# A decoder mixer: TensorE's order written into the source by counted distances, and own buffers for the decode state update

## The chip, the core and the metric

The kernel runs on one core of a Trainium2 chip. The metric is the device time of one execution in microseconds (us). Before the change three runs took 2486.36, 2490.62 and 2491.24 us; the median is 2490.62 us.

The engines go by their short names: PE (TensorE) multiplies matrices, DVE (VectorE) and ACT (ScalarE) do the elementwise work, POOL (GpSimd) a little of it and part of the DMA issues, SP (SyncE) issues the loads of weights. Each engine works through its own list of instructions in order. They meet through semaphores.

## What is computed

One inference step of one decoder layer for a prompt of 256 tokens and 8 single-token samples, together 264 columns. The layer is a half-step FFN, the mixer, attention to a memory, and a second half-step FFN. The change lies in the mixer:

```python
def mixer_block(h, pos, conv_buf, s0, swa_fn, lp):
    proj = h @ lp['w_in']
    qkv_c, z, b_raw, a_raw, q_s, k_s, v_s, gate_gdn, gate_swa = jnp.split(proj, offsets, -1)
    qkv_c, conv_new = causal_conv(qkv_c, conv_buf, lp['conv_w'])
    ...
    q_g = l2_normalize(q_g.reshape(B, T, GDN_HEADS, GDN_DK)) * (GDN_DK ** -0.5)
    k_g = l2_normalize(k_g.reshape(B, T, GDN_HEADS, GDN_DK))
    beta = jax.nn.sigmoid(b_raw.astype(jnp.float32))
    g = -jnp.exp(lp['gdn_A_log']) * jax.nn.softplus(a_raw + lp['gdn_dt_bias'])
    o_g, s_new = gated_delta_rule(q_g, k_g, v_g, g, beta, s0)
    o_g = rms_norm(o_g, lp['gdn_norm']) * jax.nn.silu(z)
    q_s, k_s = rope(q_s, pos), rope(k_s, pos)
    o_s, k_buf_new, v_buf_new = swa_fn(q_s, k_s, v_s, lp['swa_sinks'])
    merged = sigmoid(gate_gdn) * (o_g @ lp['w_br_gdn']) + sigmoid(gate_swa) * (o_s @ lp['w_br_swa'])
    return merged @ lp['w_out'], s_new, conv_new, k_buf_new, v_buf_new
```

For the prompt the gated delta rule is solved in chunks: for each pair of heads a chain of small matrix products, with a triangular inverse in the middle. For a sample it is one step, S = a(I - b k k^T)S + b k v^T, on a state of 128x128 per head and sample, which is read from HBM, updated and written back.

## The kernel before

**Weights.** Every weight matmul is done in three passes of half precision: weights and input are split into a high and a low part, and wh·xh, wh·xl and wl·xh are added up in PSUM (lines 192, 193, 194). Weights come in blocks of 512 KB: a DMA into `raw` (SP, 4 buffers), a cast by ACT into `wh` (line 162, 3 buffers), and the rest by DVE into `wl` (line 163, 4 buffers). A block feeds 24 matmuls of 128x264. A `wh` buffer is written again when the last matmul of the block three earlier is done.

**Mixer.** Between these stand the small steps. The combined input projection is computed in groups: `gemm_ba` (32 columns for beta and decay, lines 351 to 417), four pairs of GDN heads ("c0" to "c3": `conv_pair` computes k, q, v and z of a pair, `gdn_pair` solves the prompt's chunks, `gdn_sample` does the decode step), the window attention's projection ("s"), its prompt heads in four groups ("w0" to "w3") and its samples ("x"), and 16 gate groups. All of the mixer's evacuations multiply by `R`, the inverse root of the mean square of the input, which PE, DVE and a chain of small DVE operations produce at its start (lines 1234, 1237, 149 to 155; `rsqrt` is an integer estimate and three Newton steps).

**Small steps.** A step is one to sixteen matmuls or transposes on PE, whose result goes through ACT or DVE before the next step of the same chain. In `gdn_pair`: transposes of q, k and v (lines 489, 495, 513), decay matrices (519 to 526; the tiles `d`, `E1`, `E2`), k·k and q·k (531, 536), the inverse in four rounds (`sq`, `d`, lines 548 to 568) and two larger ones (580 to 600), the outputs (604 to 630), their norm (635 to 643) and the transposes of the result (646). In `gdn_sample`: the states are loaded into the tiles `d`, `T`, `U` and `bv` (line 661 on), multiplied (689), reduced and turned (695, 710), the new vectors go through HBM (`ud`, 714) and come back spread over all partitions into `ke` or `u` (728), POOL multiplies them by k (729), ACT scales the state (732), POOL adds (733) and stores (734).

**Order.** The framework's scheduler sets the order of the instructions on every engine from its own model of times; the source gives the order in which work becomes known to it. PSUM holds 3 banks for weight groups (`mm`), 2 for GDN steps (`gd`), 2 for window attention (`sw`) and 1 for the rest (`ev`).

## Time and profile before

| what | value |
|---|---|
| three runs, median | 2490.62 us |
| the profiled execution | 2495.04 us, span 2493.3 us |
| granted clock of PE, mean | 0.987 of full |
| PE busy | 2443.0 us, 98% |
| DVE busy | 1516.3 us, 61% |
| ACT busy | 1101.2 us, 44% |
| POOL busy | 111.3 us, 4% |
| HBM | 182 GB/s over the span |

The first FFN takes the span to about 790 us, the mixer from there to about 1600, the memory attention and the second FFN the rest. The small steps lie between 790 and 1365 us. The profile has views by engine, by stretch of time, by wait, and the list of instructions with their start times; the rows that are used stand two sections below.

### The profile page before, as it was taken

How to read it: one execution, taken by the hardware profiler on the slowest of the kernel's cores; microseconds unless marked ns; L12 is line 12 of the kernel's file. 1: busy time of each engine (PE TensorE's matmuls, PEld its weight loads, DVE VectorE, ACT ScalarE, POOL GpSimd, SP SyncE). 2: the span in 40 equal slices, each digit the busy share in tenths (PEclk: the TensorE clock that was granted, in tenths of full speed). 3: DMA queues.
4: the chain of work that ended last, by engine and by line, in shares of the span. 5: the costliest groups of instructions: out<-in, count | busy, mean ns of one | idle time of the engine just before them, and what ended most of it. 6: DMA issues, size and time to landing. Idle time of an engine off the chain costs nothing.

```text
span 2493.3 us, 47847 instructions
## 1 busy us (share of the span) xinstructions
PE 2443.0 (98%) x19804; PEld 2392.9 (96%) x19804; DVE 1516.3 (61%) x2555; ACT 1101.2 (44%) x1647; POOL 111.3 (4%) x159
## 2 busy tenths in 40 slices
PE   8999999999999999999998999999999999999997
PEld 8999999999999999998997999979999999999997
DVE  6555544555556877877575777668555544555554
ACT  5444333444444544554463455446444333444443
POOL 0000000000000002002020310000000000000000
PEclk9999999999999999998998999999999999999999
DMA  6555555555556457544453876755555556555553
GB/s 210 182 178 179 178 179 184 182 180 178 178 179 205 147 167 232 170 162 165 136 190 127 270 229 198 240 196 178 180 183 180 174 182 186 178 181 183 175 171 130
DMA packets 136090, 455.20 MB, mean 183 GB/s; under 512 B 16736, under 2 KB 22976, under 8 KB 135824
## 3 DMA queue, kind: packets, MB, share of 16 engines
q1 hardware_dynamic: 127072, 424.18, 53.7%
q0 software_dynamic: 7504, 24.65, 2.8%
q8 instruction: 155, 2.54, 0.4%
q10 hardware_dynamic: 1296, 3.31, 0.4%
q14 instruction: 63, 0.52, 0.1%
HBM read 438.02 MB, written 14.98 MB: 182 GB/s over the span
## 4 chain that ended last, share of the span: by engine, by line
PE 94%; DVE 3%; DMA 1%; ACT 1%; issue 1%; POOL 0%; ACTq 0%; SPq 0%; DVEq 0%; POOLq 0%
PE mm L192 18%; PE mm L194 18%; PE mm L193 18%; PE mx L194 11%; PE mx L192 11%; PE mx L193 11%; DVE wl L163 1%; DMA raw<-in_w_in_dram 1%; PE sw L812 1%; PE mm L1003 0%; ACT wh L162 0%; PE mm L1005 0%; PE mm L1004 0%; PE sw L839 0%; DMA d<-in_state_gdn_dram 0%
## 5 line engine op out<-in xcount | busy, mean ns | idle before, releaser
L163 DVE TENSOR_TENSOR wl<-raw,wh 128x1024 fp32r<-128x1024 f32 (+2 forms) x794 | 958.0, 1207 | 762.3 <-ACT wh L162 756.8
L162 ACT CAST wh<-raw 128x1024 fp32r<-128x1024 f32 (+2 forms) x794 | 817.3, 1030 | 1212.4 <-PE mm L193 611.8
L192 PE MATMUL mm<-xh,wh 128*128 128x264 f32 x2672 | 769.7, 289 | 14.2 <-ACT wh L162 10.9
L194 PE MATMUL mm<-xh,wl 128*128 128x264 f32 x2672 | 766.8, 288 | 3.1 <-DVE wl L163 3.0
L193 PE MATMUL mm<-xl,wh 128*128 128x264 f32 x2672 | 768.7, 288 | 0.0
L192 PEld LDWEIGHTS mm<-xh,wh 128*128 128x128 f32 x2672 | 508.9, 191 | 18.7 <-ACT wh L162 11.1
L194 PEld LDWEIGHTS mm<-xh,wl 128*128 128x128 f32 x2672 | 507.5, 190 | 7.4 <-DVE wl L163 4.6
L193 PEld LDWEIGHTS mm<-xl,wh 128*128 128x128 f32 x2672 | 508.7, 190 | 5.0 <-issue 3.8
L192 PE MATMUL mx<-xh,wh 128*128 128x264 f32 x1424 | 407.2, 286 | 0.3 <-DVE sso L719 0.3
L194 PE MATMUL mx<-xh,wl 128*128 128x264 f32 x1424 | 407.1, 286 | 0.3 <-DVE wl L163 0.3
L193 PE MATMUL mx<-xl,wh 128*128 128x264 f32 x1424 | 406.1, 285 | 0.0
L192 PEld LDWEIGHTS mx<-xh,wh 128*128 128x128 f32 x1424 | 270.7, 190 | 0.5 <-DVE sso L719 0.4
L194 PEld LDWEIGHTS mx<-xh,wl 128*128 128x128 f32 x1424 | 270.0, 190 | 0.6 <-DVE wl L163 0.6
L193 PEld LDWEIGHTS mx<-xl,wh 128*128 128x128 f32 x1424 | 270.1, 190 | 0.0
L194 PE MATMUL mm<-hh,wl 128*128 128x264 f32 x748 | 212.7, 286 | 0.0
L192 PE MATMUL mm<-hh,wh 128*128 128x264 f32 x748 | 212.4, 284 | 0.0
L193 PE MATMUL mm<-hl,wh 128*128 128x264 f32 x748 | 212.3, 284 | 0.0
L194 PE MATMUL mx<-hh,wl 128*128 128x264 f32 x660 | 187.6, 285 | 0.0
L192 PE MATMUL mx<-hh,wh 128*128 128x264 f32 x660 | 187.5, 284 | 0.0
L193 PE MATMUL mx<-hl,wh 128*128 128x264 f32 x660 | 187.4, 284 | 0.0
L193 PEld LDWEIGHTS mm<-hl,wh 128*128 128x128 f32 x748 | 140.9, 188 | 0.0
L192 PEld LDWEIGHTS mm<-hh,wh 128*128 128x128 f32 x748 | 140.6, 188 | 0.0
(562 smaller groups left out, 2867.0 us busy)
## 6 DMA issues: line engine op xcount, KB each, us to landing
raw<-in_ffn_w_dram SPq DMA_DIRECT2D x511, 512.0 KB, 3.5
raw<-in_w_in_dram SPq DMA_DIRECT2D x152, 512.0 KB, 3.6
raw<-in_w_out_dram SPq DMA_DIRECT2D x32, 512.0 KB, 3.7
raw<-in_ffn_w_dram SPq DMA_DIRECT2D x33, 256.0 KB, 2.7
raw<-in_w_br_gdn_dram SPq DMA_DIRECT2D x16, 512.0 KB, 5.0
raw<-in_w_br_swa_dram SPq DMA_DIRECT2D x16, 512.0 KB, 4.8
gd<-gt POOLq DMA_DIRECT2D x32, 132.0 KB, 3.0
tg<-gd POOLq DMA_DIRECT2D x32, 132.0 KB, 4.6
```

What stands on the lines that cost most here:

```text
L162: nc.scalar.copy(out=H, in_=raw)
L163: nc.vector.tensor_tensor(out=L, in0=raw, in1=H.bitcast(F32), op=ALU.subtract)
L192: nc.tensor.matmul(acc, wh, xh, start=(kg + c == 0), stop=False)
L193: nc.tensor.matmul(acc, wh, xl, start=False, stop=False)
L194: nc.tensor.matmul(acc, wl, xh, start=False, stop=(kg + c == nk - 1))
L812: nc.tensor.matmul(ps[j % 2][:, a // 2], self.qr[half, 2 * g + j // 2, qs], self.kd[g][half, 0:W], start=True, stop=True)
```

## The change

- PE's order. While `te.on` is set, each matmul and transpose is kept on PE in the order of the source. The order on DVE, ACT, POOL and SP is still the scheduler's.
- Lanes. `gdn_pair`, `gdn_sample`, `gemm_ba`, `swa_prompt` and `swa_sample` become generators. `gemm` calls `tick()` after every three weight matmuls; at a tick at most one step of one lane is put into the program, and not sooner than two ticks after the last. A bare `yield` asks for 7 ticks (lane A: GDN and `gemm_ba`), 8 (lane B: window attention) or 6 (lane V: the transposes of v) to the next step, a number asks for so many.
- Program. "c0 c1 s w0 w1 c2 w2 w3 g2 x c3 g10" takes the place of "c0 c1 s c2 w0 c3 w1 x w2 w3" and 12 gate groups. `gemm_ba` now follows k of the first pair, and its steps start 24 ticks later.
- Decode state update. The states go into `S0`, `S1`, `E1`, `bv`. `ub` gets two buffers of its own. The multiplication by k moves from POOL (16 of 128x512) to ACT (64 of 128x128). The states are loaded in `gdn_pair`.
- Smaller edits: `rsqrt` loses one DVE operation; `kb` is copied from PSUM by ACT first; the transposes of v move behind q·k; rotated queries are written in place into `os`; the caches of `swa_sample` are loaded some steps ahead.

```diff
+        self.te = InOrder(tc)
+        self.clock, self.last, self.lanes = 0, 0, []
...
-        nc.vector.tensor_scalar(out=v, in0=v, scalar1=-0.5, scalar2=None, op0=ALU.mult)
         for it in range(3):
-            nc.vector.tensor_tensor(out=t, in0=y, in1=y, op=ALU.mult)
+            nc.vector.scalar_tensor_tensor(out=t, in0=y, scalar=-0.5, in1=y, op0=ALU.mult, op1=ALU.mult)
...
+                    self.te.matmul(acc, wl, xh, start=False, stop=(kg + c == nk - 1))
+                    self.tick()
...
+    def tick(self):
+        self.clock += 1
+        ready = [n for n in self.lanes if n.todo and n.at <= self.clock]
+        if ready and self.clock >= self.last + 2:
+            min(ready, key=lambda n: n.at).step()
+            self.last = self.clock
...
-                self.gemm_ba(win, xs)
                 self.conv_state_load()
-                for step in "c0 c1 s c2 w0 c3 w1 x w2 w3".split():
+                self.te.on = True
+                A, B, V = self.lanes = [Lane(self, 7), Lane(self, 8), Lane(self, 6)]
+                self.lane_v = V
+                A.add(self.gemm_ba(win, xs), 24)
+                for step in "c0 c1 s w0 w1 c2 w2 w3 g2 x c3 g10".split():
                     k = int(step[1:] or 0)
                     if step[0] == "c":
-                        self.conv_pair(win, xs, k)
-                        self.gdn_pair(k)
-                        self.gdn_sample(k)
+                        A.drain(2)
+                        q = self.conv_pair(win, xs, k)
+                        A.add(self.gdn_pair(k, q))
+                        A.add(self.gdn_sample(k, q))
...
         ot = self.gt("d")
         TT(out=ot, in0=po, in1=bc(rn, P), op=ALU.mult)
+        yield 18
...
-                S = self.gt(("d", "T", "U", "bv")[h * 2 + hb])
+                S = self.gt(("S0", "S1", "E1", "bv")[h * 2 + hb])
...
-                ub = self.gt(("ke", "u")[hb])
+                ub = self.mc.tile([P, 4, P], F32, name="ub", bufs=2)
...
-                nc.gpsimd.tensor_tensor(out=ub, in0=ub, in1=bc(kq[:, h, hb, :, 0], P), op=ALU.mult)
                 for b in range(4):
                     bb = hb * 4 + b
+                    nc.scalar.mul(out=ub[:, b], in_=ub[:, b], mul=kq[:, h, hb, b, 0:1])
                     nc.scalar.mul(out=S[:, b], in_=S[:, b], mul=self.sbg[:, 1, 2 * p + h, bb:bb + 1])
...
             pT = mc.tile([P, nh, blk + 1, P], F32, name="pT")
+            yield 18
...
+class InOrder:
+    def matmul(self, *a, **k):
+        ins = self.tc.nc.tensor.matmul(*a, **k)
+        return self.tc.keep_in_program_order(ins) if self.on else ins
...
+class Lane:
+    def add(self, gen, wait=0):
+        if not self.todo:
+            self.at = max(self.at, self.b.clock + wait)
+        self.todo.append(gen)
+
+    def step(self):
+        try:
+            n = next(self.todo[0])
+            self.at = self.b.clock + (n or self.gap)
+        except StopIteration:
+            self.todo.pop(0)
```

What this does to the order is shown at three places.

**Place 1, PE at the mixer's start.** `mm_8952` and `mm_9064` are `gemm_ba`'s sums, the matmul with `nacc` is the one that `R` begins with, `mm_9079` and `mm_9080` before and `mm_8967` and `mm_8968` after are k of the first pair, `mm_9227` and `mm_9174` the group that follows. Before:

```order
L364 MATMUL mm_8952<-xl_8914,wh_8948 32x264
L194 MATMUL mm_9080<-xh_7797,wl_9083 128x264
L192 MATMUL mm_9079<-xh_7975,wh_9112 128x264
L1234 MATMUL ev_8986<-nacc_7608,ones_74 128x264
L193 MATMUL mm_9079<-xl_7976,wh_9112 128x264
...
L194 MATMUL mm_9080<-xh_8913,wl_9173 128x264
L369 MATMUL ev_9006<-idn_73,cy_8985 128x32
L370 MATMUL ev_9006<-idn_73,cy_8985 128x32
L371 MATMUL ev_9006<-idn_73,cy_8985 8x32
L192 MATMUL mm_9227<-xh_7604,wh_9230 128x264
```

After:

```order
L1332 MATMUL mm_9064<-xl_8913,wh_9060 32x264
L1332 MATMUL ev_9099<-nacc_7607,ones_74 128x264
L1332 MATMUL mm_8967<-xh_8718,wh_9119 128x264
...
L1332 MATMUL mm_8968<-xh_8912,wl_9120 128x264
L1332 MATMUL mm_9174<-xh_7603,wh_9177 128x264
```

Before, 71 weight matmuls stood between the matmul that `R` begins with and the first PE instruction that needs `R` (the transposes of `cy`); now 24 stand between it and `mm_9174`, which is written into the bank that an evacuation with `R` must empty first.

**Place 2, DVE around the norm of pair 0's output.** `d_9915` before and `d_10618` after is the normed output that PE then transposes; `wl_11619` is of the block that PE is in the middle of at that step, `wl_10837` of the third block behind the one that PE ends on there. Before:

```order
L154 TENSOR_TENSOR got_9901<-got_9901,so_9892 128x4
L751 TENSOR_TENSOR cth_11455<-cth_11455,c_8940 128x264
L752 TENSOR_TENSOR cy_11453<-cy_11453,c_8940 128x264
...
L163 TENSOR_TENSOR wl_11619<-raw_11617,wh_11618 128x1024
L778 TENSOR_TENSOR qr_11029<-cy_11463,cth_11465 128x264
L153 TENSOR_TENSOR got_9901<-goy_9900 128x4
...
L641 TENSOR_TENSOR rn_9893<-rn_9893,tq_9894 128x4
L643 TENSOR_TENSOR d_9915<-gd_9877,rn_9893 128x512
```

After:

```order
L154 SCALAR_TENSOR_TENSOR got_10605<-goy_10604 128x4
L164 TENSOR_TENSOR wl_10837<-raw_10835,wh_10836 128x1024
L812 TENSOR_TENSOR kd2_10652<-cy_10643,cth_10645 64x264 x2
L812 TENSOR_TENSOR kd3_10656<-cy_10643,cth_10645 64x264
L155 TENSOR_TENSOR got_10605<-got_10605,so_10596 128x4
L812 TENSOR_TENSOR kd3_10656<-cy_10643,cth_10645 64x264
...
L156 SCALAR_TENSOR_TENSOR rn_10597<-got_10605,goy_10604 128x4
L681 TENSOR_TENSOR rn_10597<-rn_10597,tq_10598 128x4
L683 TENSOR_TENSOR d_10618<-gd_10581,rn_10597 128x512
```

On PE, 115 weight matmuls stood between the last product of that pair and these transposes, and 54 stand there now. The 54 end with the last that read `wh_10693`, whose buffer `wh_10836` takes.

**Place 3, PE at the end of pair 3.** `gd` and `T`, `U`, `bv`, `S` are that pair's steps, `mm` a gate. Before, where no weight matmul stands between the first and the last of these rows:

```order
L599 MATMUL gd_13760<-Pm_13758,T_13729 64x64 x4
L604 MATMUL gd_13767<-bv_13615,U_13730 128x128 x2
L608 MATMUL gd_13771<-U_13730,kb_13608 128x128 x2
L614 MATMUL gd_13777<-u_13766,ke_13606 128x128 x2
...
L628 MATMUL gd_13794<-u_13766,ke_13606 128x128 x2
L646 MATMUL gd_13827<-idn_73,d_13825 128x128 x4
L680 MATMUL gd_13851<-pr_13843,ones_74 128x48
L689 MATMUL gd_13873<-d_13833,w_13841 32x512
...
L717 MATMUL gd_13905<-stt_13887,ones_74 128x16
```

After:

```order
L1332 MATMUL mm_15325<-xh_7974,wl_15365 128x264
L1336 MATMUL gd_15388<-idn_73,d_15295 128x128 x4
L1332 MATMUL mm_15325<-xh_7982,wh_15364 128x264
...
L1332 MATMUL mm_15520<-xh_8346,wl_15607 128x264
L1336 MATMUL gd_15614<-idn_73,su2_15548 16x128
L1332 MATMUL gd_15621<-stt_15549,ones_74 128x16
L1332 MATMUL mm_15520<-xh_8354,wh_15606 128x264
```

The steps of pair 3 that stood back to back now have weight matmuls of gates between them, and gate matmuls also follow the last of them.

## Rows read from the trace of the kernel before

**Rows 1.** The page: busy us, share of the span, instructions.

```profile
PE 2443.0 (98%) x19804; PEld 2392.9 (96%) x19804; DVE 1516.3 (61%) x2555; ACT 1101.2 (44%) x1647; POOL 111.3 (4%) x159
```

**Rows 2.** Busy time by stretch: PE, PEld, DVE, ACT, POOL, clock, DMA share, GB/s.

```profile
700.00:750.00 50.00, 50.00 (x412) 50.00 (x411) 27.94 (x37) 22.07 (x31) 0.00 (x0) 1.00 0.58 182
800.00:850.00 50.00, 45.97 (x354) 45.39 (x353) 40.07 (x104) 24.23 (x44) 0.00 (x0) 0.93 0.52 160
1100.00:1150.00 50.00, 45.73 (x328) 42.05 (x329) 43.06 (x131) 29.61 (x69) 12.58 (x13) 0.90 0.44 140
1150.00:1200.00 50.00, 50.00 (x403) 46.95 (x402) 29.43 (x68) 19.68 (x45) 6.49 (x12) 0.86 0.50 168
1350.00:1400.00 50.00, 40.49 (x286) 37.51 (x287) 36.96 (x92) 23.78 (x51) 19.10 (x23) 0.83 0.53 179
```

**Rows 3.** PE's waits: tile, line, releaser; us in total, times, longest.

```profile
PE gd L646 <- DVE d L643: 5.0, 1, 5.0
PE ev L369 <- DVE cy L366: 4.0, 1, 4.0
PE mm L192 <- DVE cy L912: 3.3, 2, 2.6
PE gd L689 <- DMA d<-in_state_gdn_dram: 3.1, 2, 2.5
PE mm L194 <- DVE wl L163: 3.0, 4, 1.2
PE gd L710 <- DVE su L705: 2.0, 2, 1.0
PE gd L695 <- DVE sq L693: 1.7, 1, 1.7
```

**Rows 4.** DVE's list at the start: start us, us, line, operation.

```profile
797.22 0.43 DVE L1237 TENSOR_SCALAR nsq<-ev 128x264 f32<-128x264 f32 x1 [3.41 <-PE ev L1234]
797.80 1.23 DVE L163 TENSOR_TENSOR wl<-raw,wh 128x1024 fp32r<-128x1024 f32 x1 [0.16 <-ACT wh L162]
...
808.92 0.43 DVE L155 SCALAR_TENSOR_TENSOR R<-nsq,nacc 128x264 f32<-128x264 f32 x1
809.39 0.42 DVE L366 TENSOR_TENSOR cy<-mm,R 32x264 f32<-32x264 f32 x1
```

**Rows 5.** DVE's list, norm of pair 0's output.

```profile
946.59 0.61 DVE L630 SCALAR_TENSOR_TENSOR S<-S,gend,gd 128x128 f32<-128x128 f32 x2 [1.00 <-PE gd L628]
...
955.51 0.43 DVE L751 TENSOR_TENSOR cth<-cth,c 128x264 f32<-128x264 f32 x1 [2.77 <-DMA cth<-cy]
955.86 0.43 DVE L752 TENSOR_TENSOR cy<-cy,c 128x264 f32<-128x264 f32 x1
...
959.75 0.16 DVE L641 TENSOR_TENSOR rn<-rn,tq 128x4 f32<-128x4 f32 x1
959.94 0.69 DVE L643 TENSOR_TENSOR d<-gd,rn 128x512 f32<-128x512 f32 x1
```

**Rows 6.** All engines' list, pair 0's decode step and state update.

```profile
975.69 0.27 PE L710 MATMUL gd<-idn,su 128*16 128x128 f32 x1
...
978.29 1.05 ACT L162 CAST wh<-raw 128x1024 fp32r<-128x1024 f32 x1 [2.03 <-PE mm L193]
...
996.62 0.57 POOL L734 DMA_DIRECT2D out_gdn_s_dram<-U  x1
```

**Rows 7.** DMA issues: KB each, median us to landing.

```profile
out_gdn_s_dram<-U POOLq DMA_DIRECT2D x4, 256.0 KB, 4.6
```

**Rows 8.** All engines' list, one softmax of the window attention.

```profile
1205.79 0.70 PE L812 MATMUL sw<-kd,qr 64*128 64x256 f32 x2
...
1213.73 0.91 ACT L828 ACTIVATE sc<-sc,sm_s 128x256 f32<-128x256 f32 x2
```

**Rows 9.** All engines' list, a subtraction on DVE beside a multiplication on POOL.

```profile
1141.73 1.05 POOL L729 TENSOR_TENSOR ke<-ke,w 128x512 f32<-128x512 f32 x1
...
1141.77 2.11 DVE L163 TENSOR_TENSOR wl<-raw,wh 128x1024 fp32r<-128x1024 f32 x1 [0.50 <-ACT wh L162]
```

More of the change, by code (lines that the diff above doesn't have):

```diff
@@ L413, in gemm_ba @@
         nc.vector.tensor_tensor(out=dg[:, 1], in0=bc(gs, NS), in1=i8, op=ALU.mult)
+        yield
         pb = self.evt()
-        nc.tensor.matmul(pb[:, 0:128], self.ones[0:NS, :], dg.rearrange("p a h b -> p (a h b)"), start=True, stop=True)
+        self.te.matmul(pb[:, 0:128], self.ones[0:NS, :], dg.rearrange("p a h b -> p (a h b)"), start=True, stop=True)
         self.sbg = mc.tile([P, 2, 8, NS], F32, name="sbg")
@@ L607, in gdn_pair @@
         for h in range(2):
-            nc.tensor.matmul(pw[:, h], kb[:, h], U[:, 2 * h + 1], start=True, stop=True)
+            self.te.matmul(pw[:, h], kb[:, h], U[:, 2 * h + 1], start=True, stop=True)
         w = self.gt("w", 2)
@@ L678, in gdn_sample @@
         TT(out=v2(pr[:, 2]), in0=kk, in1=qq, op=ALU.mult)
+        yield
         ps = self.gdt()
-        nc.tensor.matmul(ps[:, 0:3 * n], self.ones, pr.rearrange("p a b -> p (a b)"), start=True, stop=True)
+        self.te.matmul(ps[:, 0:3 * n], self.ones, pr.rearrange("p a b -> p (a b)"), start=True, stop=True)
         ss, rr, dq = st("sss", 2 * n), st("srr", 2 * n), st("sdq")
@@ L716, in gdn_sample @@
         pn = self.gdt()
-        nc.tensor.matmul(pn[:, 0:n], self.ones, t, start=True, stop=True)
+        self.te.matmul(pn[:, 0:n], self.ones, t, start=True, stop=True)
         so, rn = st("sso"), st("srn")
@@ L811, in swa_prompt @@
                 half = slice(64 * (j % 2), 64 * (j % 2) + 64)
[L812 removed]
+                self.te.matmul(ps[j % 2][:, a // 2], self.qr[half, 2 * g + j // 2, qs], self.kd[g][half, 0:W], start=True, stop=True)
             mask = self.K(C_W1 + P) if blk == 0 else self.K(C_W1, 2 * P)
@@ L859, in swa_sample, with keys @@
                 nc.vector.tensor_copy(out=knT[half(q), t, :], in_=self.kd[2 * t + q][half(q), sc])
-        ps = self.swt()
-        for b2 in range(0, NS, 2):
+        def keys(b2):
             kc = self.kc_tile()
@@ L865, in swa_sample, with values @@
             nc.vector.tensor_copy(out=kT[:, :, :, 0].rearrange("p b t -> p t b"), in_=knT[:, :, b2:b2 + 2])
-            for b in (b2, b2 + 1):
-                for t in range(2):
-                    nc.tensor.matmul(ps[:, b * 16 + t * 8:b * 16 + t * 8 + 8], kT[:, b - b2, t], qb[:, b, t], start=True, stop=True)
+            return kT
+        def values(b2):
+            vc = self.kc_tile()
+            nc.sync.dma_start(out=vc, in_=i["cache_v"][:, b2:b2 + 2])
+            nc.gpsimd.dma_start(out=vc[0:1], in_=self.vn[b2:b2 + 2, :])
+            return vc
+        kTs, vcs = [keys(b2) for b2 in (0, 2, 4)], []
+        yield 24
+        ps = self.swt()
+        for n in range(4):
+            if n:
+                yield
+            for b in (2 * n, 2 * n + 1):
+                for t in range(2):
+                    self.te.matmul(ps[:, b * 16 + t * 8:b * 16 + t * 8 + 8], kTs[n][:, b % 2, t], qb[:, b, t], start=True, stop=True)
+            if n == 0:
+                kTs.append(keys(6))
+            else:
+                vcs.append(values(2 * n - 2))
         sp2 = mc.tile([P, 2, P], F32, name="kcT", bufs=2)
@@ L890, in swa_sample @@
         po = self.swt()
-        for b2 in range(0, NS, 2):
-            vc = self.kc_tile()
-            nc.sync.dma_start(out=vc, in_=i["cache_v"][:, b2:b2 + 2])
-            nc.gpsimd.dma_start(out=vc[0:1], in_=self.vn[b2:b2 + 2, :])
-            for b in (b2, b2 + 1):
+        for k in range(4):
+            yield 16 if k == 3 else None
+            for b in (2 * k, 2 * k + 1):
                 for t in range(2):
                     n = b * 16 + t * 8
-                    nc.tensor.matmul(po[:, n:n + 8], vc[:, b - b2, t * P:(t + 1) * P], pT[:, n:n + 8], start=True, stop=True)
+                    self.te.matmul(po[:, n:n + 8], vcs[k][:, b % 2, t * P:(t + 1) * P], pT[:, n:n + 8], start=True, stop=True)
+            if k == 0:
+                vcs.append(values(6))
         for par in range(2):
@@ L983, in mem_prep @@
             for b in range(2):
-                nc.tensor.matmul(ps[:, b:b + 1], acc[:, b * P:(b + 1) * P], self.ones[:, 0:1], start=True, stop=True)
+                self.te.matmul(ps[:, b:b + 1], acc[:, b * P:(b + 1) * P], self.ones[:, 0:1], start=True, stop=True)
             v = sp.tile([P, 2], F32, name="mv_", bufs=1)
@@ L1058, in s_scores @@
             for n in range(2):
-                self.pin(nc.tensor.matmul(qb, row[:, b:b + 1].to_broadcast([NS, P]), qs[n], start=(n == 0), stop=(n == 1)))
+                self.pin(self.te.matmul(qb, row[:, b:b + 1].to_broadcast([NS, P]), qs[n], start=(n == 0), stop=(n == 1)))
             TT(out=kc, in0=kc, in1=bm(qb, 2), op=ALU.mult)
@@ L1233, in finish @@
         R = self.R = b.cst.tile([P, TOK], F32, name="R", bufs=2)
-        nc.tensor.matmul(ps[:, :TOK], b.ones, self.acc, start=True, stop=True)
+        b.te.matmul(ps[:, :TOK], b.ones, self.acc, start=True, stop=True)
         v, t = (b.cst.tile([P, TOK], F32, name="nsq", bufs=2) for _ in range(2))
```

267 lines of the change are left out of this document (159 added, 108 removed).

## The prediction

> **What bounds the kernel now.** I read the page first: PE is busy for 2443.0 of 2493.3 us [rows 1], so only what PE loses can be won. The table by stretch shows where. In a stretch of the FFN 412 matmuls start in 50 us, one every 0.121 us, at clock 1.00 [rows 2]; that pace is the floor for weight matmuls. In the mixer four stretches have a lower granted clock: 0.93, 0.90, 0.86 and 0.83, which is time at the lower of its two levels (1.2 instead of 2.4 GHz). A mean of 0.83 over 50 us is 50 x 0.17 = 8.5 us of full-speed work not granted; the four make 3.5 + 5.0 + 7.0 + 8.5 = 24.0 us. Next the view of PE's waits [rows 3]: seven lines, 5.0 + 4.0 + 3.3 + 3.1 + 3.0 + 2.0 + 1.7 = 22.1 us, all for a DVE result but one, a state load. Together 46 us, about 1.8% of the time. A little is counted twice, where PE waits while the clock is low. All else on PE is work that the change keeps. So 46 us is the ceiling, and no faster time than about 2491 - 46 = 2445 us can come of it.
>
> **What the change takes away.** The end of pair 3 has its steps back to back because no gate matmuls were left (place 3); there the 5.0, most of the 3.1, the 1.7 and half of the 2.0 us of [rows 3] are lost, and the 8.5 us of clock behind them. Now gates stand between and behind the steps: those 19 us go. The waits and the clock of 1100 to 1200 (12.0 us of clock, 2.6 us for L912) belong to an old order with bursts of small matmuls, which is broken up: I count them gone too. The start's 4.0 and 3.5 us I take out and price anew. So I subtract all 46 and add what the new order makes PE wait. One operation fewer in each `rsqrt`, the move of v's transposes, `kb` and the rotated queries in place cost nothing on PE; they lie on DVE and ACT, and are in the sums below where they stand in front of a waiting step.
>
> **What the change adds.** A counted distance covers a chain with weight matmuls at 0.121 us each. It can't see what DVE has in its queue, whose order stays the scheduler's. For each step I sum the rows of DVE and ACT that stand in front of its input, and subtract its cover.
>
> Start. `mm_9174` needs the bank that the first evacuation with `R` empties, 24 matmuls or 2.9 us behind the matmul that `R` begins with (place 1). Before, that way took DVE from 797.22 to 809.39, 12.2 us, behind 71 matmuls (8.6 us), and 4.0 us of wait were left [rows 3, 4]. In the new order nine dependent Newton operations at 0.47 (start to start, [rows 4]) are 4.2 us, two `wl` at 1.23 are 2.5, eight other operations together 1.9: 8.6 us, less 2.9 is **5.7**. Bounds: twelve dependent operations alone, 5.6 - 2.9 = 2.7; the old way whole, 12.2 - 2.9 = 9.3. The next step of `gemm_ba` has 21 matmuls instead of 48 in front; its sum leaves **2.4** (0 if the clock is low then).
>
> Norm of pair 0. 54 matmuls cover 6.6 us, where there were 115 (place 2). On DVE `wl_10837` stands in front of the rest; it needs the cast of `wh_10836`, which can begin only when PE has read the last of `wh_10693`, with the 54th matmul. So nothing of what follows is covered: cast 1.05 [rows 6], `wl` 1.23, four `kd` operations at 0.35 (start to start as in [rows 5]) = 1.4, six dependent small ones at 0.20 (959.75 to 959.94) = 1.2, eight others at 0.1 = 0.8, the output 0.69: **6.4**. Bounds: before, the chain took from 946.59 to 960.63, 14.0 us, 7.4 over the cover; at pair 3, with an idle DVE, PE waited 5.0 us with no cover at all [rows 3], so it could also be nothing. I take the sum, because the buffer ties it to PE. The same step of the other pairs, summed alike: 2.7, 1.3, 0.8, in all **4.8**.
>
> State update. `E1` holds the third of sample 0's states, and pair 1, which follows at once, needs `E1` for its decay matrix. Before, that store was issued 996.62 - 975.69 = 20.9 us behind PE's transposes of the update and needed 4.6 us to land [rows 6, 7], 25.5 us. From there to the step that needs it, the mask, the exponential, four products and the first inverse round's inputs are some 4 us. PE's cover is 153 weight matmuls and some 24 small ones, 21 us. That leaves 8; POOL no longer multiplies, ACT does, which I set against each other but for 1 us: **7**. It is 5 if ACT is quick, 9 if it is late.
>
> Softmax. Its transposes come 54 matmuls behind the scores, with the small steps between about 7.6 us; before, the chain took 1205.79 to 1214.64, 8.9 us [rows 8]. Twelve such steps: 0 to 12 x 1.3 = 15.6. Summed by queue, four wait: 4.5, 2.8, 1.6, 0.8, **9.7**.
>
> Five small ones (first inverse round of pair 0 2.5, and 0.4 to 1.0 each at four others): **5.5**. The waits added: 5.7 + 2.4 + 6.4 + 4.8 + 7 + 9.7 + 5.5 = 41.5 us.
>
> Clock. Behind the 4.0 us of wait at 806 the stretch lost 3.5 us of clock [rows 2, 3]. Four of the new waits are as long (start, norm of pair 0, `E1`, the first softmax): 14; less 2, since the wait of 2.4 falls into such a stretch: **12**.
>
> Added 53.5, removed 46: **+7 us**. Against the profiled execution (2495.04) that is about 2502; it lay 4.4 us over the median, so on the scale of the runs 2490.6 + 7 = 2498 us. I call 0.2%, 5 us, what a measurement can tell from no change.
>
> **A rule beside the trace.** In [rows 9] a `wl` beside a POOL multiplication took 2.11 us; alone it took 1.23 [rows 4]. The Trainium skill (GPSIMD Engine Reference, 1. Specifications) says that POOL shares its SBUF interfaces with VectorE and contends with instructions that have two SBUF inputs, as `wl` has. The trace agrees in that row. The price in rows: sixteen multiplications leave POOL, at most 16 x 0.88 = 14 us of DVE time; I count none of it above, because the long sums are made of waits for the cast, the store and dependent operations.
>
> **Rivals.**
> - Faster, the queues are shorter than I sum. DVE is busy for at most 43 of 50 us in these stretches [rows 2], so it may be ahead at the steps. Then the norms and softmaxes are covered, as pair 3's 5.0 us against 6.6 allow, and what is left is the start at 2.7, `E1` at 5 and small ones of 7, with two drops of clock, 7: 22 against 46, 2467 us. Against it: place 2, where the cast is bound to PE itself. It decides at the wait before pair 0's transposes: under 2 us.
> - Faster by a little, DVE freed from POOL: up to 14 us less than my sum, 2484.
> - About the same: the waits are as summed, but spread so that the clock holds, or half of the softmax waits fall away: 53.5 - 8 = 45.5 against 46, 2490. It decides by the number of drops of clock: one or two.
> - Slower by more, ACT becomes late. It gets 64 activations for 16 POOL operations; eight more for one state between two casts are 2.4 us at an estimated 0.3 each (twice as wide ones take 0.46, [rows 8]); a late cast makes a late `wl` and PE waits in the weight stream. With one such stall for each pair 4 x 2.4 = 10 more: 2508. It decides if PE waits for `wl` or `wh` by over 5 us in all.
> - The change doesn't do what it says: PE's list is in the order of the source (places 1 and 3), so only the distances can fail, and that is my forecast.
>
> **How the numbers follow.** Forecast 0.33, ACT late 0.12, about the same 0.27, shorter queues 0.22, DVE freed 0.06. Slower by over 0.2%: 0.45; within: 0.27; faster: 0.28. The forecast's own range, by the bounds of start, `E1` and softmax, is 2496 to 2508. To leave out no more than 2 in 10 it must reach down into the shorter queues (2467 is that case's centre) and up past late ACT: 2468 to 2514.
>
> **What would show it.** Right: waits of 5 to 7 us for `R`, before pair 0's transposes and before pair 1's inverse, a clock under 0.95 behind each, none left around the end of pair 3. Wrong: less than 25 us of waits on PE in the mixer, or DVE idle in front of the long ones.

## The result, and the profile after

The changed kernel takes 2520.58 us (median of four runs, 2520.17 to 2521.66) against 2489.28 before (2486.36 to 2491.24, four runs): a ratio of 1.0123, interval 1.0110 to 1.0135. It is slower by 31 us. The forecast was slower by 7, and 2520.6 lies outside its range. The profiled execution took 2521.66 us, its span is 2519.9; against the profiled execution of before that is 26.6 us more.

The page shows the same number of matmuls, and PE busy for 5.2 us less in a span that is 26.6 us longer. ACT is busy for 20.1 us more and POOL for 23.2 less, as the multiplications by k moved from one to the other, and DVE for 15.8 less. To read with [rows 1]:

```profile
PE 2437.8 (97%) x19804; PEld 2389.8 (95%) x19804; DVE 1500.5 (60%) x2533; ACT 1121.3 (44%) x1715; POOL 88.1 (3%) x143
```

The table by stretch, columns as in [rows 2]. Before, PE was busy for 45.97 us in 800 to 850 and for 47.5 to 50 in the five stretches behind it:

```profile
800.00:850.00 50.00, 42.04 (x308) 40.70 (x307) 37.59 (x97) 21.30 (x39) 0.00 (x0) 0.90 0.42 129
900.00:950.00 50.00, 42.46 (x360) 41.26 (x359) 33.70 (x82) 17.80 (x28) 2.72 (x5) 0.94 0.52 158
950.00:1000.00 50.00, 41.28 (x313) 39.81 (x311) 32.49 (x96) 23.34 (x52) 10.71 (x14) 0.91 0.58 185
1000.00:1050.00 50.00, 43.28 (x380) 40.04 (x381) 32.76 (x73) 18.48 (x37) 0.06 (x1) 0.88 0.50 155
1350.00:1400.00 50.00, 48.22 (x390) 47.40 (x389) 29.32 (x45) 28.68 (x57) 14.79 (x22) 1.00 0.78 249
```

The end of pair 3 is mended: 1350 to 1400 has 48.22 us of PE at clock 1.00, where it had 40.49 at 0.83. The loss is new in 800 to 1050. PE's waits between 780 and 1400 us, columns as in [rows 3]:

```profile
PE gd L1336 <- DVE d L578: 11.9, 1, 11.9
PE gd L1336 <- DVE d L683: 11.6, 4, 7.5
PE sw L1336 <- ACT sc L888: 11.4, 5, 5.9
PE gd L1336 <- DVE E L559: 5.5, 2, 2.8
PE mm L1332 <- DVE sq L384: 5.5, 1, 5.5
```

All lines of this view together are 23.8 us before and 54.4 after. L683 is the norm's output, L888 the softmax, L384 the first evacuation that needs `R`, L578 the first inverse round of pair 1, L559 the product behind which the transposes of v find their bank.

I also read the clock's records in both traces. Between 790 and 1420 us PE has 47.8 us at the lower clock before and 58.0 after. A third account puts each distance between two starts on PE against the median of its shape at full clock, from 800 to 1400 us: 81.2 us lost before, 107.2 after. The 26.0 more are nearly the whole difference of 26.6. By kind they are about +28.9 in waits, +1.8 at low clock outside of them and -5.0 in the small steps themselves, together 25.7; the parts, though not the sum, shift by 1 to 2 us with the shortest gap that is called a wait.

The short rows. Start, DVE's list, as [rows 4]: from `nsq` to the first use of `R` it is 7.8 us where it was 12.2.

```profile
804.05 0.43 DVE L1320 TENSOR_SCALAR nsq<-ev 128x264 f32<-128x264 f32 x1 [0.68 <-PE ev L1332]
...
811.89 0.42 DVE L384 TENSOR_TENSOR sq<-mm,R 32x264 f32<-32x264 f32 x1
```

Norm of pair 0, ACT's list, then DVE's, as [rows 5]: the cast that needs PE's last matmul, its `wl`, `kd` in threes, the output; between the last two lies the small chain.

```profile
940.83 1.04 ACT L163 CAST wh<-raw 128x1024 fp32r<-128x1024 f32 x1 [1.90 <-PE mm L1332]
```

```profile
942.64 1.22 DVE L164 TENSOR_TENSOR wl<-raw,wh 128x1024 fp32r<-128x1024 f32 x1
943.77 1.32 DVE L812 TENSOR_TENSOR kd<-cy,cth 64x264 f32<-64x264 f32 x3
...
947.70 0.69 DVE L683 TENSOR_TENSOR d<-gd,rn 128x512 f32<-128x512 f32 x1
```

Pair 0's state update, as [rows 6, 7], first PE's transposes of the update, then POOL's list (`E` is `E1`: the views leave out the numbers of names). Three stores of old caches and old convolution state stand just ahead of `ud`:

```profile
966.43 0.27 PE L1336 MATMUL gd<-idn,su 128*16 128x128 f32 x1
```

```profile
966.93 0.61 POOL L843 DMA_DIRECT2D out_k_old_dram<-in_cache_swa_k_dram  x1
967.53 0.58 POOL L843 DMA_DIRECT2D out_v_old_dram<-in_cache_swa_v_dram  x1
968.11 0.54 POOL L844 DMA_DIRECT2D out_conv_old_dram<-in_state_conv_dram  x1
968.64 0.54 POOL L764 DMA_DIRECT2D ud<-sut  x1
...
995.40 1.26 POOL L783 TENSOR_TENSOR E<-E,ub 128x512 f32<-128x512 f32 x1 [2.45 <-ACT ub L781]
996.95 0.56 POOL L784 DMA_DIRECT2D out_gdn_s_dram<-E  x1 [0.30 <-POOL E L783]
```

SP's list, then ACT's and DVE's: the load of `ub` stands behind eight rotary copies, ACT for `ub`, DVE for the store of `E1`.

```profile
971.88 10.44 SPq L800 DMA_DIRECT2D cth<-cy  x8
982.42 0.53 SPq L162 DMA_DIRECT2D raw<-in_w_in_dram  x1
983.04 0.85 SPq L778 DMA_DIRECT2D ub<-ud  x2
```

```profile
987.97 2.45 ACT L781 ACTIVATE ub<-ub,w 128x128 f32<-128x128 f32 x8 [6.24 <-DMA ub<-ud]
```

```profile
1001.07 0.69 DVE L544 SCALAR_TENSOR_TENSOR E<-d,c 128x512 f32<-128x512 f32 x1 [1.11 <-DMA out_gdn_s_dram<-E]
...
1005.59 0.29 DVE L578 TENSOR_TENSOR d<-c,sq 128x128 f32<-128x128 f32 x1
```

### The profile page after: what moved, and what is told of

Same layout as the page of the kernel before. It is cut to its first block, busy times and chain, and to the rows that moved or that the text cites. A ratio compares the mean times of both kernels' runs of the same rounds, so it can differ in the third digit from the quotient of the medians.

```text
span 2519.9 us, 47882 instructions
## 1 busy us (share of the span) xinstructions
PE 2437.8 (97%) x19804; PEld 2389.8 (95%) x19804; DVE 1500.5 (60%) x2533; ACT 1121.3 (44%) x1715; POOL 88.1 (3%) x143
## 4 chain that ended last, share of the span: by engine, by line
PE 89%; issue 5%; DVE 3%; DMA 2%; ACT 1%; POOL 0%; ACTq 0%; SPq 0%; DVEq 0%; POOLq 0%
PE mm L1332 52%; PE mx L1332 33%; PE gd L1332 1%; DVE wl L164 1%; DMA ub<-ud 1%; PE ap L1332 1%; PE sw L1332 1%; ACT wh L163 1%; DMA raw<-in_w_in_dram 0%; PE gd L1336 0%; DMA x<-in_x_dram 0%; PE sw L1336 0%; DVE cy L454 0%; PE fps L1336 0%; ACT ub L781 0%
## 5 line engine op out<-in xcount | busy, mean ns | idle before, releaser
L1332 PE MATMUL mm<-xh,wh 128*128 128x264 f32 (+1 forms) x2688 | 788.3, 294 | 17.3 <-ACT wh L163 11.8
L1332 PE MATMUL mm<-xl,wh 128*128 128x264 f32 (+1 forms) x2688 | 771.1, 287 | 0.7 <-DVE xl L1308 0.7
L1332 PEld LDWEIGHTS mm<-xh,wh 128*128 128x128 f32 (+1 forms) x2688 | 514.2, 191 | 30.7 <-issue 13.9
L1332 PEld LDWEIGHTS mm<-xl,wh 128*128 128x128 f32 (+1 forms) x2688 | 513.4, 191 | 1.2 <-DVE xl L1308 1.0
```

What stands on the lines that cost most here:

```text
L1332: ins = self.tc.nc.tensor.matmul(*a, **k)
```

## The experiments

"Waits" is the sum of PE's waits from 780 to 1400 us, "half clock" the time at the lower clock from 790 to 1420; both of the profiled run.

| kernel | waits | half clock | median us | ratio to before, interval |
|---|---|---|---|---|
| before | 23.8 | 47.8 | 2489.28 | 1 |
| changed | 54.4 | 58.0 | 2520.58 | 1.0123 (1.0110 to 1.0135) |
| e8 free order | 21.8 | 23.9 | 2484.76 | 0.9989 (0.9979 to 0.9998) |
| e12 free, POOL multiplies, T and U | 23.8 | 30.7 | 2486.50 | 0.9986 (0.9977 to 0.9995) |
| e7 before, ACT multiplies | 27.2 | 34.1 | 2492.28 | 1.0016 (1.0006 to 1.0026) |
| e9 fixed from the last gates on | 28.0 | 41.0 | 2496.77 | 1.0028 (1.0016 to 1.0039) |
| e10 as e9, POOL multiplies, T and U | 32.7 | 47.8 | 2500.46 | 1.0040 (1.0027 to 1.0052) |
| e2 norm distance 30 | 57.3 | 64.9 | 2526.74 | 1.0154 (1.0137 to 1.0171) |
| e3 softmax distance 30 | 53.4 | 68.3 | 2519.86 | 1.0128 (1.0113 to 1.0143) |
| e11 all distances longer | 40.2 | 44.4 | 2513.86 | 1.0093 (1.0076 to 1.0111) |
| e4 `gemm_ba` first | 58.9 | 58.0 | 2522.79 | 1.0137 (1.0122 to 1.0152) |
| e1 states in T, U | 45.7 | 47.8 | 2510.81 | 1.0089 (1.0074 to 1.0104) |
| e5 POOL multiplies | 59.8 | 61.4 | 2524.50 | 1.0144 (1.0129 to 1.0159) |
| e6 both | 42.4 | 44.4 | 2503.16 | 1.0060 (1.0045 to 1.0075) |
| e13 rotary copies on POOL | 53.6 | 61.4 | 2519.25 | 1.0117 (1.0101 to 1.0133) |
| e17 cache stores later | 47.9 | 44.4 | 2511.60 | 1.0091 (1.0074 to 1.0108) |
| e18 e17 with T, U | 46.0 | 41.0 | 2510.18 | 1.0083 (1.0068 to 1.0098) |
| e14 free, pair 3 earlier | 17.2 | 17.1 | 2478.15 | 0.9952 (0.9934 to 0.9970) |
| e15 free, all pairs first | 31.4 | 47.8 | 2507.07 | 1.0069 (1.0053 to 1.0085) |
| e16 e14's program, fixed | 74.3 | 85.3 | 2549.19 | 1.0235 (1.0219 to 1.0251) |

### Is it the fixed order, or the other edits?

```diff
-                self.te.on = True
```

> The changed kernel, but PE is not held to the order of the source; the lanes still give the order in which the work becomes known. Theory D (the fixed order itself is what costs, since the scheduler can no longer move a step behind its input): below 2500 us. Rival (the distances in the source, the tile and the multiplication on ACT are what costs, and stay): 2510 to 2522 us.

Without the fixed order, and with all else as changed, the kernel is faster than before by some 3 us. So the fixed order costs 33 to 36 us, and the other edits together bring some 3. The free order has its loss where before had it, at the end of pair 3; PE is idle there and the clock falls:

```profile
1300.00:1350.00 50.00, 42.16 (x352) 38.05 (x351) 26.32 (x68) 16.27 (x30) 3.78 (x7) 0.93 0.44 135
1350.00:1400.00 50.00, 47.14 (x360) 45.88 (x360) 32.28 (x67) 30.76 (x65) 16.01 (x25) 0.93 0.69 229
```

Beside it, ACT's multiplication in the kernel before:

```diff
-                nc.gpsimd.tensor_tensor(out=ub, in0=ub, in1=bc(kq[:, h, hb, :, 0], P), op=ALU.mult)
                 for b in range(4):
                     bb = hb * 4 + b
+                    nc.scalar.mul(out=ub[:, b], in_=ub[:, b], mul=kq[:, h, hb, b, 0:1])
```

> The kernel before, with one edit of the change alone: ACT multiplies the update by k in 64 operations, in ke and u as before. Theory C: ACT stands still for ke and u in four places and the weight stream or a small step behind it waits: 2494 to 2505 us. Rival (in the old order the scheduler keeps them clear of what is urgent): 2486 to 2491 us.

It costs 0.16%, and 2492.28 us lies between the two expectations. And the reverse of this diff in the free order (e8), with `("S0", "S1", "T", "U")` for the states:

> e8 (free order), with the multiplication by k back on POOL and the states in T and U. If these two matter only since the order is fixed: within 3 us of e8, 2482 to 2488 us. If they cost by themselves: 2470 to 2478 us.

That is the time of e8: neither edit counts while PE may take other work. The order fixed only at the end:

```diff
-                self.te.on = True
...
+                    self.te.on = self.te.on or step == "g10"
```

> The changed kernel with the free order of e8 up to the last ten gate groups; from there on PE keeps the order of the source, which reaches back to about the second half of the window attention. Theory D (a fixed order costs where DVE and ACT are behind, and pays where the weight matmuls run out, at the end of pair 3): the end of pair 3, 12 us of waits and 13.7 us of low clock in e8, goes; the waits of the changed kernel behind 1200 (about 7 us) come back: 2470 to 2477 us. Rival (the fixed part costs as much as it saves): 2483 to 2488 us.

It is 0.3% slower than before, outside both expectations. Start and tail were as hoped, but where the fixed part begins 1150 to 1200 has 31.7 us of PE at a mean clock of 0.62: 198 instructions of PE stand in these 50 us, where the stretch before has 400, and only 12 of them are weight matmuls. I take it that the free part had drawn these forward. With POOL multiplying and the states in `T`, `U` as well (e10, expected 2 to 4 us below e9, or within 2) it was 2500.46 us, 3.7 above e9, with the same jam.

### Are the distances too short?

```diff
         TT(out=ot, in0=po, in1=bc(rn, P), op=ALU.mult)
-        yield 18
+        yield 30
```

> The changed kernel, but 30 ticks (90 weight matmuls) in place of 18 (54) before the transposes of the normed output. Theory A (each distance is too short by itself): 36 more matmuls cover 4.4 us; the waits for d L683, 7.5 + 2.6 + 1.2 + 0.3 = 11.6 us, come down to about 3.1, the low clock behind 943 shrinks by 3 us: about 2509 us. Rival B (the DVE list is made anew and the wait moves to the next step of the same chain): 2518 to 2521 us.

> The changed kernel, but 30 ticks in place of 18 before the transposes of the softmax of the window attention. Theory A (each distance is too short by itself): the waits for sc L888, 11.4 us, come down to about 1.5, and two drops of the clock behind them (1107 and 1169, 3 us each) go: about 2505 us. Rival B (the wait moves on): 2518 to 2521 us.

The second has the same edit at the softmax. PE's waits in the first, then in the second:

```profile
PE sw L1336 <- ACT sc L888: 22.1, 8, 4.9
PE gd L1336 <- DVE d L578: 16.3, 1, 16.3
PE mm L1332 <- DVE sq L384: 5.5, 1, 5.5
PE gd L1336 <- DVE d L683: 4.9, 1, 4.9
```

```profile
PE gd L1336 <- DVE d L683: 14.9, 3, 7.5
PE gd L1336 <- DVE d L578: 11.7, 1, 11.7
PE sw L1336 <- ACT sc L888: 7.7, 1, 7.7
```

The wait that got the longer distance shrinks (11.6 to 4.9, 11.4 to 7.7), and others grow: in e2 by more (all waits 57.3 us, 54.4 in the changed kernel), in e3 by somewhat less (53.4), with 10 us more at the lower clock. The time of e3 is its rival's; e2 is slower than either expectation. So the waits move on. Why they do was not traced; I take it that a longer distance at one step brings the steps of another lane, or the next of this one, nearer to their inputs. All distances longer by about a third, with 30 at norm and softmax:

```diff
-                A, B, V = self.lanes = [Lane(self, 7), Lane(self, 8), Lane(self, 6)]
+                A, B, V = self.lanes = [Lane(self, 9), Lane(self, 10), Lane(self, 8)]
...
-            yield 14 if n == 0 else None
+            yield 18 if n == 0 else None
```

> The changed kernel with every counted distance longer by about a third (7, 8, 6 ticks become 9, 10, 8; 18 become 30; 14 become 18), all of PE's order still fixed. Theory E (the distances are too short, all together): the waits of the changed kernel, about 58 us, fall to 25, but steps of pair 3 are left over at the end and run back to back as before the change, 12 us and 8 of clock: 2500 to 2508 us. Theory D (with a fixed order the waits move to other steps whatever the distance): 2515 to 2528 us.

It gains 7 us, between the two expectations (its runs lie 10 us apart, and the profiled one is the fastest), and the tail comes back: 1350 to 1400 has 43.1 us of PE at clock 0.86, since pair 3 ends after the gates. And `gemm_ba` ahead of the first pair, as before the change:

```diff
+                for _ in self.gemm_ba(win, xs):
+                    pass
...
-                A.add(self.gemm_ba(win, xs), 24)
```

> The changed kernel, but with gemm_ba in front of the first pair again, outside the fixed order, as before the change. Theory A: the waits for sq L384 (5.5 us) and before gg (2.5 us) become the one of before (4.0 us), and 10.2 us of low clock become 6.8: 5.5 us gained, about 2515 us. Rival B (the chain through R is as long as before and only its place changes): 2519 to 2521 us.

No gain: the wait for `R` is 7.7 us instead of 5.5 there.

### Why pair 1 waits 12 us

The states of the third and fourth group out of `E1`, `bv`:

```diff
-                S = self.gt(("S0", "S1", "E1", "bv")[h * 2 + hb])
+                S = self.gt(("S0", "S1", "T", "U")[h * 2 + hb])
```

> The changed kernel, but the third and fourth decode state lie in T and U, which the chain of the prompt has done with, and no longer in E1 and bv. Theory A (E1 is held by the state until its store has landed, and PE waits for that in the next pair): the waits for d L578 (11.9 us) and for E L559 (5.5 us) and the low clock at 988 to 1012 fall away, 17.4 us of waits and 6 of clock, about 2497 us. Rival B (the update of the state is late because its loads and the multiplications on ACT stand in line behind other work; the late queue holds up everything, the tile only shows it): PE waits in the same 980 to 1010 for wl or wh instead, 5 us gained at most, 2515 us.

It gains 10 us, between the two expectations; the gap before pair 1's inverse falls from 12.0 to 2.2 us, with 3.4 behind it. The waits for L559 stay (5.3 us in two), so these are not for `E1`, as theory A had it. The multiplication back on POOL (the reverse of the diff of e7), alone and then with `T`, `U`:

> The changed kernel, but POOL multiplies the update by k again (16 operations), in the two buffers of its own. Theory C (ACT stands still for the loads of ub: 26.3 us of idle time at L781, 11 times, in front of casts, exponentials and the softmax, so the steps of pair 1 and the first softmax wait for the line on ACT): no more idle time on ACT for ub, the waits around 984 to 1006 and at 1103 shrink by about half, 12 to 18 us gained, 2503 to 2508 us. Rival A (only the counted distances and the tile E1 matter): 2518 to 2522 us.

> The changed kernel with both edits, POOL multiplies again and the states lie in T and U. Theory C with E1: both gains add, 10 from the tiles and 12 to 18 from the multiplication, 2492 to 2499 us. Rival (both shorten the same wait of pair 1): no better than the better one of the two, 2503 to 2510 us.

Alone it gives nothing, against theory C: the softmax waits fall to 6.7 us, but the store of `E1` comes later still (issued at 1003.40 us; L578: 24.8 us in two waits). With `T`, `U` it gives 7 us beyond e1, and the time is the rival's. So ACT's 64 multiplications do cost in the fixed order: ACT stands for `ub`, 26.3 us in 11 waits between 790 and 1400 us, with softmax and casts queued behind.

Why `ub` came late I first read off SP's list, and tried:

```diff
-                nc.sync.dma_start(out=t[r:r + 32], in_=y[r ^ 32:(r ^ 32) + 32])
+                nc.gpsimd.dma_start(out=t[r:r + 32], in_=y[r ^ 32:(r ^ 32) + 32])
```

> The changed kernel with the copies of rotated queries and keys issued by POOL and not by SP; all else as changed. Theory (SP's queue): in the changed kernel eight such copies hold SP from 971.9 to 982.4 us, and the load of ub stands behind them; ACT then waits 6.2 and 2.7 us for ub, and the store of the third state, which pair 1's decay matrices need, comes that much later. Without them on SP, PE's wait before pair 1's inverse falls from 12.0 + 3.0 us to 5 to 8 in all, with 3 us of clock: some 2510 us. Rival (the store alone: POOL's own queue and the 4.6 us that a store takes): the wait stays over 11 us, and the copies that now stand on POOL in front of the state's addition and store may make it longer: 2520 to 2526 us.

My theory fell: 2519.25 us, just under the rival's range. With SP free, the load of `ub` was issued at 979.5 instead of 983.0 us, and PE waited 15.9 us in one piece. What was left in front of `ub` was `ud` itself: 8 KB, from issue to landing 10.9 us here and 11.6 in the changed kernel, against 1.6 before. The views of DMA issues, before (930 to 985 us) and changed (962 to 985); KB, median us to landing:

```profile
out_k_old_dram<-in_cache_swa_k_dram POOLq DMA_DIRECT2D x1, 1016.0 KB, 9.9
ud<-sut POOLq DMA_DIRECT2D x1, 8.0 KB, 1.6
```

```profile
out_k_old_dram<-in_cache_swa_k_dram POOLq DMA_DIRECT2D x1, 1016.0 KB, 9.5
out_v_old_dram<-in_cache_swa_v_dram POOLq DMA_DIRECT2D x1, 1016.0 KB, 10.7
out_conv_old_dram<-in_state_conv_dram POOLq DMA_DIRECT2D x1, 192.0 KB, 11.7
ud<-sut POOLq DMA_DIRECT2D x1, 8.0 KB, 11.6
```

Before, the three stores were issued from 937.56 us on, 39 us ahead of `ud` (976.54); now 1.7 us ahead. `ud` landed at 968.64 + 11.6 = 980.2, just behind the last of them (968.11 + 11.7 = 979.8). So they alone were moved behind the update:

```diff
         def store():
...
-                for nm, src in (("k_old", "cache_swa_k"), ("v_old", "cache_swa_v")):
-                    nc.gpsimd.dma_start(out=o[nm], in_=i[src][:, 1:P])
-                nc.gpsimd.dma_start(out=o["conv_old"], in_=i["state_conv"][:, 1:3, :])
...
                 nc.gpsimd.dma_start(out=o["gdn_s"][2 * p + h, :, hb * 4:hb * 4 + 4], in_=S)
+        if p == 0:
+            with self.tc.issue_after(ins.ins):
+                for nm, src in (("k_old", "cache_swa_k"), ("v_old", "cache_swa_v")):
+                    nc.gpsimd.dma_start(out=o[nm], in_=self.i[src][:, 1:P])
+                nc.gpsimd.dma_start(out=o["conv_old"], in_=self.i["state_conv"][:, 1:3, :])
```

> The changed kernel with the three stores of old caches and old convolution state (2.2 MB from HBM to HBM) issued behind pair 0's state update on POOL, not just ahead of ud; all else as changed. Theory (these stores delay ud): ud lands in 2 to 4 us and not in 11.6, ub is issued up to 8 us sooner, ACT does not stand for it, and PE's wait before pair 1's inverse falls from 15.0 to 6 to 9 us, about the 7 of the prediction: 2510 to 2514 us. Rival (SP: the load of ub stands behind the rotary copies until 982 us whenever ud has landed): ud lands early, ub is issued no sooner than 981 us, the wait stays at 12 us or more: 2517 to 2522 us.

> The same, and the third and fourth state in T and U in place of E1 and bv. Theory (two causes that add up, late ud and the shared tile): no wait before pair 1's inverse over 2 us, the other waits as changed: 2505 to 2510 us, faster than e1_state_tiles (2510.8), which kept the late ud. Rival (with its own tiles the update is off the path, and when ud lands does not matter): the time of e1_state_tiles within 2 us.

The first came out as the theory said. `ud` landed in 3.9 us, and the wait shrank; POOL's list, then PE's waits:

```profile
967.01 0.51 POOL L764 DMA_DIRECT2D ud<-sut  x1 [0.35 <-ACT sut L762]
...
985.60 0.56 POOL L784 DMA_DIRECT2D out_gdn_s_dram<-E  x1
```

```profile
PE gd L1337 <- DVE d L578: 6.9, 2, 4.9
```

The store of `E1` is issued 11.4 us sooner than in the changed kernel, 19.4 us behind PE's transposes of the update (966.16) and not 30.5, and 8 to 9 us of the time are gone. The 4.9 us that are left before pair 1's inverse are no longer for the store: it had landed by 990.8 (5.2 us), and DVE came to L544 at 992.10 without idle time before it. The other runs bear this out. In nine kernels, all with PE's order fixed from the start, the three stores were issued at most some 3 us ahead of a `ud`, and it took 8.6 to 12.5 us to land; the other 71 `ud` of all runs took 1.6 to 5.2. The second went as its rival: e18 and e1 are the same within 0.6 us, and only 1.4 us below e17. Late `ud` and the shared tile are one chain, and it is enough to cut it in one place.

### Fixed order or place of pair 3?

```diff
-                self.te.on = True
...
-                for step in "c0 c1 s w0 w1 c2 w2 w3 g2 x c3 g10".split():
+                for step in "c0 c1 c2 s w0 c3 w1 w2 w3 x g12".split():
```

> PE's order is the scheduler's (te.on is never set), all other edits as changed, but the program is c0 c1 c2 s w0 c3 w1 w2 w3 x g12, so that pair 3 ends with some 1300 weight matmuls still to come. Theory (the loss at the end of pair 3 belongs to the place of pair 3 in the program): the waits of 5.2, 2.6, 1.4 and 0.9 us there and the 13.7 us of low clock behind them, some 18 us in the free order, go, and the other stretches lose what they lost: 2466 to 2473 us, faster than both kernels. Rival (the free order packs its small steps somewhere whatever the program says): the burst only moves to the end of another pair or of the window attention, 2482 to 2490 us.

> PE's order fixed as in the change, with the program c0 c1 c2 s w0 c3 w1 w2 w3 x g12. Theory (the fixed order pays at each counted step whose input is late, wherever it stands): waits of some 60 us and a low clock behind the long ones stay, and as there was no tail left to win, 2512 to 2530 us; pairs 1 and 2 now follow without the window attention between, so E1 is waited for twice (two waits of 8 to 12 us). Rival (the change failed by its program and not by fixing): with the program of e14_free_early3 it comes within 5 us of that kernel's time.

e16 has the program's line alone. With the scheduler's order this program is faster than both kernels, by 0.5% against before, though 2478.15 us lies between the two expectations; with the fixed order it is the slowest of all, beyond either expectation, 71 us apart on the same source but one line. The tail in the free order:

```profile
1300.00:1350.00 50.00, 48.30 (x392) 46.16 (x392) 26.89 (x85) 19.89 (x43) 6.44 (x12) 0.97 0.49 149
1350.00:1400.00 50.00, 49.72 (x407) 49.38 (x406) 34.14 (x60) 30.64 (x58) 17.02 (x27) 1.00 0.83 278
```

Two thirds of the loss that e8 has there (20.2 us in the third account; 6.7 here) is gone, less than the 18 us expected: 5 come back between 900 and 1000, where PE now waits for ACT's `qg` (3.3 us). In the fixed order:

```profile
PE sw L1336 <- ACT sc L888: 21.2, 5, 8.3
PE gd L1336 <- DVE d L578: 16.7, 2, 14.6
```

The 14.6 us stand behind another late `ud`: the three stores are issued at 1056.05 to 1057.21 us, `ud` at 1058.73, and it takes 10.2 us to land.

With all four pairs first, in the free order, the place costs time:

```diff
-                self.te.on = True
...
-                for step in "c0 c1 s w0 w1 c2 w2 w3 g2 x c3 g10".split():
+                for step in "c0 c1 c2 c3 s w0 w1 w2 w3 x g12".split():
```

> As before, but with the program c0 c1 c2 c3 s w0 w1 w2 w3 x g12: all four pairs ahead of the window attention. Theory: the tail is gone here too, but 28 small steps come in one row in PE's list near the end of the window attention, with no weight matmuls between: 5 to 10 us of waits and 7 us of low clock are left there: 2472 to 2480 us. Rival (the place does not matter): the same time as with the free order and the program of the change, 2483 to 2488 us.

It takes 2507.07 us, slower than before by 0.7% and outside both expectations. The jam came, but at 1000 to 1050 us (38.0 us of PE, mean clock 0.73) and not at the end of the window attention; place and size were not foreseen.

## Why the prediction was wrong, point by point

The sign was right, the size was not: +7 against +31. Term by term, predicted and measured (the gap on PE in the changed kernel):

| term | predicted us | measured us |
|---|---|---|
| start, `R` | 5.7 | 5.66 |
| next step of `gemm_ba` | 2.4 | 2.62 |
| norm of pair 0 | 6.4 | 7.69 |
| norms of pairs 1 to 3 | 2.7, 1.3, 0.8 | 2.65, 1.55, 0.36 |
| pair 1's inverse (`E1`) | 7 | 12.01 and 1.05 |
| softmax | 4.5, 2.8, 1.6, 0.8 | 6.08, 3.41, 1.58 |
| first inverse round of pair 0 | 2.5 | 2.52 |
| transposes of v, pairs 1 and 3 | 0 | 2.96, 2.87 |
| clock, new less old | 12 - 24 = -12 | +1.8 (third account), +4.5 (table of stretches) |

**What held.** Sums of DVE's and ACT's rows, less the cover, gave the wait at the start within 0.1 us, and the norms and the later softmaxes within 1.3. At the norm of pair 0 the size is in part luck. The sum tied DVE to PE by the cast that waits for PE's 54th matmul, and that is what decided against the faster rival. The cast came as said, from 940.83 to 941.87, but DVE reached its `wl` only at 942.64, with no idle time before it: the cast held up nothing. From 938 to 948.4 us DVE stood nowhere for 0.15 us or more; PE waited for the length of DVE's list alone, in which other work took the place of the 1.05 us of the cast. The tail of pair 3 went as said: in the third account the 1300s lost 24.2 us before and lose 4.7.

**The state update: the step that failed is the 20.9 us from PE's transposes of the update to the store, taken over from before.** From PE's transposes of the update (966.43) to the store of `E1` it is 996.95 - 966.43 = 30.5 us, not 20.9, and to the step that had waited for it 34.6, not 25.5. From there to pair 1's inverse it is 4.9 us, near the 4 of the sum. What PE has in between is 27.7 us (to 994.09), not 21, with the earlier gap of 2.8 us in it. So 25.5 - 1 + 4 - 21 = 7.5 became 34.6 + 4.9 - 27.7 = 11.8. The runs put the cause of the late store in the three stores that the new order on POOL sets just ahead of `ud` (e17: 19.4 us instead of 30.5, and 8 to 9 us of time), and not, as I thought after seeing the trace, in SP's queue (e13). Nor was it "POOL no longer multiplies, ACT does, which I set against each other but for 1 us": with POOL multiplying (e5) the store comes later still. I had moved the window projection's steps in the sum by their PE, DVE and ACT rows, and not by the DMAs they issue.

**The transposes of v: the step that failed is "the move of v's transposes, `kb` and the rotated queries in place cost nothing on PE".** These transposes wait for L559, 2.96 us at pair 1 and 2.87 at pair 3, with 3.4 us at the lower clock behind each. At pair 1 DVE stood for a rotary copy, with L559 behind it in its list (986.07):

```profile
982.63 0.43 DVE L801 TENSOR_TENSOR cth<-cth,c 128x264 f32<-128x264 f32 x1 [2.95 <-DMA cth<-cy]
```

With these copies issued by POOL (e13) the wait at pair 1 is gone and the one at pair 3 is left (L559: 2.8 us, once). No run moves the transposes alone.

**The softmax.** The first is 6.08 instead of 4.5: ACT's exponential stands behind multiplications that wait for `ub`, which no row of before shows since POOL did them. That is what the rival on late ACT says, but not by its mark: PE's waits for `wl` and `wh` between 780 and 1400 are under 2 us. Beside e1, e6 prices ACT's multiplications at 7 us; the softmax waits fall from 11.7 to 7.5 there.

**The clock: the step that failed is "Four of the new waits are as long (start, norm of pair 0, `E1`, the first softmax): 14".** By the table of stretches the mean clocks of after make 28.5 us of work not granted, against 24.0 before: the old loss was replaced whole, not by half. Part of that falls into the waits themselves, where it costs nothing; outside of them it is the +1.8 of the third account, against the -12 of the forecast. Behind nine gaps on PE stands a stretch at the lower clock, and not behind the four long ones alone: 6.8 us behind 5.66, 3.4 behind 2.62, 2.52, 2.96 and 2.87, 10.2 behind 7.69, 13.7 behind 12.01, 6.8 behind 6.08 and 3.41. Two of these stretches, with the clock 0.50 in the column behind POOL:

```profile
943.70:953.90 10.20, 5.46 (x25) 5.46 (x26) 5.03 (x21) 0.00 (x0) 1.07 (x2) 0.50 0.27 90
998.30:1012.00 13.70, 5.28 (x29) 4.85 (x30) 8.14 (x18) 3.12 (x7) 1.46 (x2) 0.50 0.46 147
```

Set beside the third account, the forecast was +19.4 of waits (41.5 less 22.1) - 12 of clock = +7.4; measured are +28.9 and +1.8, less 5.0 in the small steps, +25.7. So 9.5 us of the miss are waits and 13.8 the clock, and the small steps gave 5.0 back.

**The scale.** 26.6 us between the profiled executions became 31.3 between the medians, because the profiled execution of before lies 5.8 us over the median of its four runs and that of after 1.1 over its own. The profiled execution of before has a granted clock of 0.987, where the later executions of the same kernel have 0.988 to 0.991, each 0.001 worth 2.5 us; so a part of the 24 us of clock that the forecast took away was the loss of one execution. The forecast's own range, 2496 to 2508, does not come out of the bounds that it names: start, `E1` and softmax at their bounds together give 2483 to 2510. The result lies above both.

**The rivals.** Shorter queues (2467) fell with the norm: 7.69 us there, not under 2. About the same (2490) fell with the clock: nine drops, not one or two. DVE freed from POOL: the Trainium skill (GPSIMD Engine Reference, 1. Specifications) says that POOL shares its SBUF interfaces with VectorE, and the traces agree in sign, though the effect is small: `wl` takes 1279 ns on average before and 1246 after (950 to 1400 us, 108 and 105 of them), 1233 where ACT multiplies in the kernel before (e7) and 1263 where POOL multiplies again (e5). From before to after that is 3.5 us of DVE time, and e7 shows none of it in the time.

**What stays open.** Whether the program of e14 would bring its gain on the kernel before, without the other edits, was not tried. Nor is it settled which of the small edits makes up the 3 us of e8. With POOL multiplying and the states in `T`, `U`, the fixed order is still 17 us slower than the free one (e6 2503.16, e12 2486.50): the waits for `R`, the norms, most softmaxes and v are left there, and whether an order fixed on DVE and ACT as well would take them away was not tried.

## What to carry to other kernels

A fixed order on the engine that bounds a kernel turns a late input into idle time. Here it mended the end of pair 3 (4.7 us lost there in the third account, 20.2 with the free order of e8) and lost far more elsewhere; an earlier place of pair 3 with the order left free mended most of it too (6.7), and e14 and e16, which differ in the fixed order alone, lie 71 us apart. So if work runs out behind a chain, first move the chain in the program, and leave the order free; not every earlier place pays (e15). Where a step moves, list the DMAs that it issues and what stands behind them in their queue; and count a clock loss behind gaps of 2.5 us too, not behind the long ones alone (here behind nine of the ten gaps of 2.5 us or more).
